# Element-wise work on VectorE alone, and the last factors of the MLP's input deferred, in a two-layer decoder step

## The chip, the core and the metric

The kernel runs on one core of a Trainium2 chip. The core has four engines that compute: TensorE multiplies matrices, VectorE, ScalarE and GpSimd work element by element; SyncE issues most transfers. Each engine takes its own instructions strictly in order and waits on semaphores for the others. The metric is the device time of one execution in microseconds (us). Before the change it is 1240.17 us, the median of three runs (1239.22 to 1240.53).

## The reference

One inference step of a small decoder with two layers, on 512 prompt tokens and 8 sample tokens (520 columns), model width 1024, MLP width 4096, all in float32:

```python
def rmsnorm(x, g): return x * rsqrt(mean(x * x) + EPS) * g
def sq_relu_mlp(x, g, w_up, w_down):
    return square(relu(rmsnorm(x, g) @ w_up)) @ w_down
# mixer A: input product -> six heads of chunkwise retention, group norm and swish gate,
#          beside attention over 256 memory tokens -> output product -> residual
# MLP 0; then one shared K/V product of the stream
# mixer B: input product -> twelve heads of sliding-window attention with sinks,
#          beside attention over memory tokens -> output product -> residual
# MLP 1; final RMSNorm
```

It returns the normed stream, the retention states and the key and value caches.

## The kernel before

The stream lies in the on-chip memory as eight blocks `xs[kt]` of 128 features by 520 tokens. Every product is computed on TensorE from split numbers: a float32 operand is cast to a shorter format on ScalarE (the high half, names in `h`), and the rest is subtracted on VectorE (the low half, names in `l`); three products of halves are added up in a bank. So before each product stands a pair of a ScalarE cast and a VectorE subtraction for the weights (`chunk`, lines 205 to 217; 128x1024 each, three buffers per kind) and for the input (`Pair.put`, lines 178 to 180; `cut`, line 251). A weight tile is fetched by SyncE once the buffer of the tile three earlier is free.

The program has four stages: mixer A, MLP 0, mixer B, MLP 1, with a norm at the start of each and one at the end. A norm squares on ScalarE, adds the squares up (line 384), sums over features on TensorE, takes the root by some eleven tiny VectorE steps (lines 357 to 365) and spreads the result through TensorE.

The MLP's input `xg` is split at once for the first four output blocks, which are computed by a plain product (`DIRECT = 2` pairs). For the rest the kernel uses a seven-product scheme on 2x2 halves: `operands` makes seven combinations of the input's quarter blocks (names `f0...`, `f1...`; the factors), and `seven` makes four sums of weight quarters for each pair of output blocks (names `u...s`, line 322, 128x512; the totals), 28 times in all.

Which engine does an element-wise step is written by hand in strings: `p` means GpSimd and `v` VectorE (`ENG_W` for the totals, `ENG_R` for the norms' adds, `POOL_N` for the window softmax, `TAIL_P` for the last multiplies). The multiplies of weights by a gain (line 214, `by`) and the multiply of `q` by decay (line 606) are always on GpSimd.

The order of each engine's instructions is not that of the code. The steps are recorded by generators in an order given by strings (`ORDER_A`, `ORDER_B`), and a scheduler then sorts each engine's instructions by a simulated time of readiness when the program is built. The sorted order is fixed; on the chip each engine follows it.

Names used below: `al` is the low half of mixer A's input; `ga` and `gt` are its gates, `rx` and `ry` TensorE's turned outputs of a head, `on` and `op` the normed head, `oah`, `oal` the halves of the gated outputs (`oah1` and `oal1` hold blocks 4 to 7; block 5 is head 5), `oa0` to `oa7` the output weights. In mixer B, `kv0` to `kv3` are the weights of the shared K/V, `qb0` to `qb7` those of the queries, a name such as `kv001` is the bank of tile 0, token half 1, and `kvb`, `qb1` are what the banks are evacuated to (line 421). `bms` are the norm's sums, `br` its spread result. `wp` are the window softmax's weights, six heads in turn (line 705). In the MLPs, `hid` also holds the split `xg`, `u` is an output block of the first product and `d` one of the second.

Of the kernel before, what the change touches and what calls it, by code (L numbers as in the profile page):

```python
# [33 lines left out]
DIRECT = 2  # L34
UK = KT // 2
# [11 lines left out]
ENG_UL = "vvvvvvvv"  # L47
ENG_R = dict(a='ppppvppv', m='pppppppv', f='vvvvvvvv', b='vvvvvpvv', y='vppppppv')
ENG_B = "pvvvvvvv"
ENG_W = "pvppppvp"  # L50
# [6 lines left out]
TAIL_P = (3, 5, 7)  # L57
STORES = ((1, 3, 5, 7), (0, 2, 4, 7))
KEEP = 4
POOL_W = (1, 4, 5)  # L60
POOL_N = (0, 1)
# [56 lines left out]
def build(tc, d, o):  # L118
    nc = tc.nc
    with ExitStack() as ctx:  # L120
# [39 lines left out]
        class Pair:  # L160
# [44 lines left out]
        def chunk(src, n, name, place=None, eng=nc.vector, by=None):  # L205
# [45 lines left out]
        def cut(op, j, src, eng):  # L251

            h, l = op[:, 0, j, :], op[:, 1, j, :]
            nc.scalar.copy(out=h, in_=src)
            eng.tensor_sub(out=l, in0=src, in1=f(h))

        def operands(name, g, scale, direct, norm):
# [12 lines left out]
            def put(i, j, src):  # L270
                if i not in op:
                    op[i] = half(f"{name}{i}", F32R, [P, 2, UK, EVEN])
                cut(op[i], j, src, nc.vector)

            for n, kt in enumerate(BY_PAIR):
                j = kt % UK
# [4 lines left out]
                if kt < UK:  # L281
                    first[j] = y
                    put(1, j, y[:, left])
                    combine(5, j, y[:, right], y[:, left], ALU.subtract)
                else:
                    b11, b12, b21, b22 = first[j][:, left], first[j][:, right], y[:, left], y[:, right]
                    t = combine(7, j, b22, b12, ALU.subtract)
                    t = combine(6, j, t, b11, ALU.add)
                    put(3, j, b22)
                    combine(4, j, b21, t, ALU.subtract)  # L290
                    put(2, j, b21)
            return op
# [819 lines left out]
```

## Time and profile before

| | us |
|---|---|
| median of three runs | 1240.17 |
| profiled execution | 1238.24 |
| its span (first to last instruction) | 1236.4 |
| TensorE busy | 1196.2 |
| VectorE busy | 833.4 |
| ScalarE busy | 534.6 |
| GpSimd busy | 229.4 |

The profile is of one execution, so that the sums below are made against its own span. Busy shares are means over stages that differ much: TensorE has nearly no idle time in the long product stretches and most of it at the boundaries of stages. The mean granted clock of TensorE over the span was 0.985 of full speed.

### The profile page before, as it was taken

To read this page: it belongs to the slowest core of one execution; us is meant where nothing else is said; L and a number is where in the kernel's file an instruction comes from. 1 tells how busy PE (TensorE), PEld (TensorE's weight loads), DVE (VectorE), ACT (ScalarE), POOL (GpSimd) and SP (SyncE) were. 2 spreads that over 40 slices of the span, in tenths; PEclk is the share of its full clock that TensorE was granted. 3 is DMA by queue.
4 is the path that set the end of the run, shared out by engine and by line. 5 is a ranking of instruction groups with operands and counts; after the bars stand their busy time and mean duration, and the time that the engine had idled before them with its cause. 6 is when DMAs were issued, how large, how long until landed. Compare 5 with 4: busy or idle time off the path is not lost. (4 is left out here: it accounts for less than half of the span.)

```text
span 1236.4 us, 23686 instructions
## 1 busy us (share of the span) xinstructions
PE 1196.2 (97%) x9718; PEld 1138.7 (92%) x9718; DVE 833.4 (67%) x1615; ACT 534.6 (43%) x999; POOL 229.4 (19%) x207
## 2 busy tenths in 40 slices
PE   8999999999999999999999998899799999999996
PEld 7999989999999999999999785579699999999996
DVE  7676777789766666675557558559796566666633
ACT  6232442355554444444324325455464444444532
POOL 2301100001312112121024114110222121121112
PEclk9999999999999999999999999899899999999998
DMA  8344622221223232232324354001132222323402
GB/s 304 112 151 168 217 77 72 88 86 71 73 97 120 86 116 91 97 106 75 121 99 143 107 163 141 30 1 68 36 103 103 82 107 86 120 86 104 140 32 69
DMA packets 43788, 128.25 MB, mean 104 GB/s; under 512 B 5112, under 2 KB 10368, under 8 KB 43552
## 3 DMA queue, kind: packets, MB, share of 16 engines
q1 hardware_dynamic: 41440, 119.80, 27.8%
q0 software_dynamic: 2240, 6.95, 1.5%
q8 instruction: 76, 1.25, 0.4%
q14 instruction: 32, 0.26, 0.1%
HBM read 117.65 MB, written 9.08 MB: 102 GB/s over the span
## 5 line engine op out<-in xcount | busy, mean ns | idle before, releaser
L438 DVE TENSOR_TENSOR xs<-d,xs 128x264 f32<-128x264 f32 (+1 forms) x128 | 54.0, 423 | 102.0 <-PE d L235 102.0
L235 PE MATMUL d<-hid,dw 128*128 128x256 f32 (+1 forms) x384 | 46.9, 283 | 0.0
L235 PEld LDWEIGHTS d<-hid,dw 128*128 128x128 f32 x384 | 46.3, 188 | 0.1
L830 ACT ACTIVATE u<-u 128x520 f32<-128x520 f32 x56 | 35.6, 636 | 21.5 <-DVE u L829 21.5
L639 POOL DMA_DIRECT2D out_ret_s<-s x12 | 6.9, 571 | 135.5 <-DVE s L638 102.8
L235 PE MATMUL ob<-obh,obw 128*128 128x256 f32 (+1 forms) x128 | 26.9, 297 | 2.4 <-ACT obh L179 1.6
L700 ACT ACTIVATE wp<-wp,wnm 128x256 f32<-128x256 f32 (+1 forms) x48 | 22.5, 469 | 12.6 <-DVE wes L697 8.6
L235 PEld LDWEIGHTS ob<-obh,obw 128*128 128x128 f32 x128 | 21.0, 193 | 5.0 <-ACT obh L179 3.0
L705 POOL TENSOR_SCALAR wp<-wp,wsm 128x256 f32<-128x256 f32 (+1 forms) x32 | 15.4, 498 | 54.8 <-ACT wp L700 28.5
L180 DVE TENSOR_TENSOR hid<-u,hid 128x520 fp32r<-128x520 f32 x32 | 23.3, 727 | 0.0
L829 DVE SCALAR_TENSOR_TENSOR u<-u,f0r 128x520 f32<-128x520 f32 x28 | 22.7, 811 | 0.4
L829 DVE SCALAR_TENSOR_TENSOR u<-u,f1r 128x520 f32<-128x520 f32 x28 | 22.7, 811 | 0.4
L524 ACT ACTIVATE p<-ms,nm 128x256 f32<-128x256 f32 x32 | 14.9, 476 | 18.5 <-DVE nm L522 16.8
L713 PEld LDWEIGHTS wt<-c,wp 128*128 128x128 f32 x84 | 9.8, 148 | 12.0 <-POOL wp L705 6.2
L179 ACT CAST hid<-u 128x520 fp32r<-128x520 f32 x32 | 20.1, 628 | 1.0
L713 PE MATMUL wt<-c,wp 128*128 128x128 f32 x84 | 15.7, 300 | 4.7 <-POOL wp L705 2.7
L235 PE MATMUL ob<-obl,obw 128*128 128x256 f32 (+1 forms) x64 | 18.1, 296 | 1.0 <-DVE obl L180 1.0
L522 DVE TENSOR_REDUCE nm<-ms 128x2 f32<-128x512 f32 x16 | 10.3, 685 | 11.8 <-PE ms L503 11.8
L180 DVE TENSOR_TENSOR obl<-wo,obh 128x128 fp32r<-128x128 f32 x24 | 6.9, 287 | 16.2 <-ACT obh L179 16.2
L503 PE MATMUL ws<-kvb,qb 64*128 64x256 f32 (+1 forms) x96 | 15.6, 407 | 1.2 <-DVE wp L690 0.6
L715 ACT COPY wpT<-wt 128x384 f32<-128x384 f32 x28 | 12.8, 479 | 8.2 <-PE wt L713 7.8
L690 DVE SCALAR_TENSOR_TENSOR wp<-cb,ws 128x256 f32<-128x256 f32 (+1 forms) x48 | 15.4, 375 | 0.1
(1997 smaller groups left out, 5124.6 us busy)
## 6 DMA issues: line engine op xcount, KB each, us to landing
kc<-in_mem_k SPq DMA_DIRECT2D x16, 256.0 KB, 4.1
vc<-in_mem_v SPq DMA_DIRECT2D x16, 256.0 KB, 4.4
s<-in_S SPq DMA_DIRECT2D x12, 256.0 KB, 4.9
out_ret_s<-s POOLq DMA_DIRECT2D x12, 256.0 KB, 2.5
xs<-in_xT SPq DMA_DIRECT2D x8, 260.0 KB, 4.3
memx<-in_memT SPq DMA_DIRECT2D x1, 1024.0 KB, 7.6
u004r<-in_w_up SPq DMA_DIRECT2D x2, 512.0 KB, 3.3
u006r<-in_w_up SPq DMA_DIRECT2D x2, 512.0 KB, 3.1
```

What stands on the lines that cost most here:

```text
L179: nc.scalar.copy(out=self.hi(kt, sl, rows), in_=src)
L180: eng.tensor_sub(out=self.lo(kt, sl, rows), in0=src, in1=f(self.hi(kt, sl, rows)))
L235: nc.tensor.matmul(t, w[:, ws], a(kt, HALVES[s]), start=kt == k[0] and m == 0, stop=kt == k[-1] and m == 2)
L438: nc.vector.tensor_add(out=x[mb][:, ts], in0=t, in1=x[mb][:, ts])
L503: i = m()
L524: nc.scalar.activation(out=t[:, b, :], in_=s[hh][:, b, :], func=AF.Exp, bias=nm[:, b:b + 1], accum_out=sm[:, b:b + 1])
L690: nc.vector.scalar_tensor_tensor(out=pv[:, j, :], in0=cb["nd"][:, k0:], scalar=float(SLOPES[6 * kb + j]), in1=sv[j // 3][j % 3], op0=ALU.m ...
L700: nc.scalar.activation(out=pv[:, j, :], in_=pv[:, j, :], func=AF.Exp, bias=nm[:, j:j + 1], accum_out=sm[:, j:j + 1])
L705: (nc.gpsimd if j % 3 in POOL_N else nc.vector).tensor_scalar(out=pv[:, j, :], in0=pv[:, j, :], scalar1=sm[:, j:j + 1], scalar2=1.0, op0=A ...
L713: nc.tensor.transpose(t[:, i * P:i * P + P], p[:, 3 * hh + i, kk * P:kk * P + P], ident)
L829: nc.vector.scalar_tensor_tensor(out=u[i], in0=u[i], scalar=0.0, in1=r[0], op0=ALU.max, op1=ALU.mult)
L830: nc.scalar.square(out=u[i], in_=u[i])
```

## The change

Two things change. All element-wise work of GpSimd goes to VectorE, with one exception: of the six heads of a window softmax, which GpSimd (four) and VectorE (two) scaled, VectorE now scales four and ScalarE two. GpSimd keeps memsets and the issue of its output transfers. The strings that chose engines are removed. Then `operands` returns the factors of its last two pairs (four blocks) as a generator, and the MLP's `up` takes one step of it behind each of the first two plain output blocks.

```diff
+LATE = 2
-ENG_UL = "vvvvvvvv"
-ENG_R = dict(a='ppppvppv', m='pppppppv', f='vvvvvvvv', b='vvvvvpvv', y='vppppppv')
-ENG_B = "pvvvvvvv"
-ENG_W = "pvppppvp"
-TAIL_P = (3, 5, 7)
-POOL_W = (1, 4, 5)
-POOL_N = (0, 1)
+ACT_N = (2, 5)
...
                 if by:
                     w = raw.rearrange("p (k c) -> p k c", k=KT)
-                    nc.gpsimd.tensor_tensor(out=w, in0=w, in1=gains[:, GAINS.index(by), :].unsqueeze(2).to_broadcast([P, KT, n // KT]),
+                    nc.vector.tensor_tensor(out=w, in0=w, in1=gains[:, GAINS.index(by), :].unsqueeze(2).to_broadcast([P, KT, n // KT]),
                                             op=ALU.mult)
...
+            def factors(j, upper, lower):
+                b11, b12, b21, b22 = (t[:, c] for t in (upper, lower) for c in (left, right))
+                put(1, j, b11)
+                combine(5, j, b12, b11, ALU.subtract)
+                t = combine(7, j, b22, b12, ALU.subtract)
+                t = combine(6, j, t, b11, ALU.add)
+                put(3, j, b22)
+                combine(4, j, b21, t, ALU.subtract)
+                put(2, j, b21)
+
+            later = []
             for n, kt in enumerate(BY_PAIR):
...
+                later.append(y)
+                if n < KT - 2 * LATE and n % 2:
+                    factors(n // 2, *later)
+                    later = []
+            return op, (factors(UK - LATE + i, *later[2 * i:2 * i + 2]) for i in range(LATE))
...
             def total(i, x0, x1, alu):
-                engine(ENG_W, i, turn).tensor_tensor(out=s[i], in0=x0, in1=x1, op=alu)
+                nc.vector.tensor_tensor(out=s[i], in0=x0, in1=x1, op=alu)
...
-                    engine(ENG_R[self.name[0]], 0 if self.direct else kt).tensor_add(out=acc, in0=acc, in1=sq)
+                    nc.vector.tensor_add(out=acc, in0=acc, in1=sq)
...
                 for j in range(6):
-                    (nc.gpsimd if j % 3 in POOL_N else nc.vector).tensor_scalar(
-                        out=pv[:, j, :], in0=pv[:, j, :], scalar1=sm[:, j:j + 1], scalar2=1.0, op0=ALU.mult, op1=ALU.mult)
+                    if j in ACT_N:
+                        nc.scalar.mul(out=pv[:, j, :], in_=pv[:, j, :], mul=sm[:, j:j + 1])
+                    else:
+                        nc.vector.tensor_scalar(out=pv[:, j, :], in0=pv[:, j, :], scalar1=sm[:, j:j + 1], scalar2=None, op0=ALU.mult)
...
-            op = operands(f"f{l}", f"mlp{l}", scale, xg, m)
+            op, late = operands(f"f{l}", f"mlp{l}", scale, xg, m)
...
                     hid.put(n, u)
+                    next(late, None)
                     yield
...
-                (nc.vector if s and kt not in TAIL_P else nc.gpsimd).tensor_mul(out=y, in0=y, in1=r)
+                nc.vector.tensor_mul(out=y, in0=y, in1=r)
```

The moves change the sorted order on every engine. Three places follow. The first is TensorE at the end of mixer A, behind the turned outputs of head 5 (`rx5`, `ry5`). Before:

```order
L667 MATMUL ry5_2914<-c_77,op5_2906 128x128
L235 MATMUL oa001_3215<-oah0_2276,oa0h_3184 128x264
L235 MATMUL oa001_3215<-oal0_2278,oa0h_3184 128x264
L667 MATMUL ry5_2914<-c_77,op5_2906 128x128
L235 MATMUL oa001_3215<-oah0_2276,oa0l_3185 128x264
L235 MATMUL oa001_3215<-oah0_2276,oa0h_3184 128x264
L235 MATMUL oa001_3215<-oal0_2278,oa0h_3184 128x264
L235 MATMUL oa001_3215<-oah0_2276,oa0l_3185 128x264
```

After, at the same place:

```order
L226 MATMUL oa400_3247<-oal1_1215,oa4h_3242 128x256
L226 MATMUL oa400_3247<-oah1_1213,oa4l_3243 128x256
L661 MATMUL rx5_2913<-c_77,on5_2905 128x128 x4
L661 MATMUL ry5_2914<-c_77,op5_2906 128x128 x2
L226 MATMUL oa000_3189<-oah1_1213,oa0h_3184 128x256
L226 MATMUL oa001_3215<-oah1_1213,oa0h_3184 128x264
L226 MATMUL oa400_3247<-oah1_1213,oa4h_3242 128x256
L226 MATMUL oa000_3189<-oal1_1215,oa0h_3184 128x256
```

Before, 31 matmuls that need other blocks follow the second `ry5`; now the last block's matmuls of three banks, which need head 5's output, follow at once. The second place is VectorE at the start of mixer B, behind the norm's last step `ry5`. Before:

```order
L365 SCALAR_TENSOR_TENSOR ry5_7952<-rqt_7956,rqu_7955 104x5
L400 TENSOR_TENSOR rz5_10326<-ry5_7952 104x5
L217 TENSOR_TENSOR kv3l_8316<-kv3r_8314,kv3h_8315 128x1024
L421 SCALAR_TENSOR_TENSOR kvb_7823<-kv000_7987,br_7968 128x256
L426 SCALAR_TENSOR_TENSOR qb1_7822<-qb1_7822,br_7968 128x520 x2
```

After:

```order
L359 SCALAR_TENSOR_TENSOR ry5_7952<-rqt_7956,rqu_7955 104x5
L205 TENSOR_TENSOR qb2r_8654<-qb2r_8654,gains_73 128x1024
L394 TENSOR_TENSOR rz5_10282<-ry5_7952 104x5
L415 SCALAR_TENSOR_TENSOR kvb_7823<-kv000_7987,br_7968 128x256
L415 SCALAR_TENSOR_TENSOR kvb_7823<-kv100_8166,br_7968 128x256
L420 SCALAR_TENSOR_TENSOR qb1_7822<-qb1_7822,br_7968 128x520 x2
```

`kv3l` has moved ahead of the norm, and the multiply of `qb2`'s weights by the gain, which was GpSimd's, now stands ahead of the evacuation of `kv000`. TensorE's sums of the norm, `bms`, stood inside the product of `kv000` before, and stand three matmuls into that of `kv100` now. The third place is VectorE at the start of MLP 1, ahead of the low half of the last block of `xg` (`f1xg7`). Before:

```order
L180 TENSOR_TENSOR hid1_10110<-f1xg3_10225,hid1_10110 128x520
L255 TENSOR_TENSOR f11_10117<-f1xg3_10225,f11_10117 128x260
L384 TENSOR_TENSOR f1acc_10111<-f1acc_10111,f1sq6_10229 128x520
L255 TENSOR_TENSOR f14_10147<-f1t41_10183,f14_10147 128x260
L266 TENSOR_TENSOR f1t62_10213<-f1t72_10209,f1xg2_10189 128x260
L255 TENSOR_TENSOR f15_10122<-f1t52_10198,f15_10122 128x260
L255 TENSOR_TENSOR f17_10134<-f1t72_10209,f17_10134 128x260
L322 TENSOR_TENSOR u104s0_10556<-u104s0_10556,u104r0_10549 128x512
L180 TENSOR_TENSOR hid1_10110<-f1xg7_10238,hid1_10110 128x520
```

After:

```order
L171 TENSOR_TENSOR hid1_10110<-f1xg3_10203,hid1_10110 128x520
L246 TENSOR_TENSOR f11_10124<-f1xg3_10203,f11_10124 128x260
L316 TENSOR_TENSOR u104s0_10556<-u104r1_10550 128x512
L378 TENSOR_TENSOR f1acc_10111<-f1acc_10111,f1sq6_10207 128x520
L316 TENSOR_TENSOR u104s1_10557<-u104r0_10549,u104r1_10550 128x512
L246 TENSOR_TENSOR f14_10147<-f1t41_10183,f14_10147 128x260
L257 TENSOR_TENSOR f1t62_10327<-f1t72_10323,f1xg2_10189 128x260
L246 TENSOR_TENSOR f15_10129<-f1t52_10319,f15_10129 128x260
L246 TENSOR_TENSOR f17_10134<-f1t72_10323,f17_10134 128x260
L171 TENSOR_TENSOR hid1_10110<-f1xg7_10210,hid1_10110 128x520
```

One total of the next product stood ahead of that low half, and needed GpSimd's two before it; now two totals stand there, both VectorE's own, and the factors keep their places.

## Rows read from the trace of the kernel before

**Rows 1.** The page's first lines: span, then busy time of each engine.

```profile
span 1236.4 us, 23686 instructions
...
PE 1196.2 (97%) x9718; PEld 1138.7 (92%) x9718; DVE 833.4 (67%) x1615; ACT 534.6 (43%) x999; POOL 229.4 (19%) x207
```

**Rows 2.** Three stretches: length, busy us (instructions) per engine, granted clock, DMA share, GB/s.

```profile
345.00:640.00 295.00, 294.95 (x2460) 294.74 (x2459) 186.44 (x240) 125.12 (x183) 52.89 (x37) 1.00 0.28 99
740.00:840.00 100.00, 86.77 (x585) 63.95 (x584) 63.59 (x200) 51.11 (x174) 23.74 (x35) 0.93 0.16 53
840.00:895.00 55.00, 46.65 (x348) 45.03 (x347) 48.41 (x104) 29.03 (x59) 7.92 (x4) 0.91 0.16 58
```

**Rows 3.** The waits of TensorE: instruction, releaser, us in total, times, longest.

```profile
PE u L235 <- DVE hid L180: 6.1, 2, 4.1
PE wt L713 <- POOL wp L705: 2.7, 5, 1.9
...
PE u110a L300 <- DVE u110l L317: 0.9, 1, 0.9
...
PE qm L235 <- DVE al L248: 0.7, 2, 0.4
```

**Rows 4.** Line 322 on VectorE: ns shortest, median, longest, then its start.

```profile
L322 DVE TENSOR_TENSOR u026s<-u026r,u026s x1: 680/680/680, 489.7 to 489.7; 128x512 f32<-128x512 f32 x1
...
L322 DVE TENSOR_TENSOR u104s<-u104s,u104r x1: 1741/1741/1741, 871.3 to 871.3; 128x512 f32<-128x512 f32 x1
```

**Rows 5.** Timeline, start of mixer B: start, us, instruction, [idle before <-releaser].

```profile
662.03 0.99 PE L394 MATMUL bms<-c,bacc 128*104 128x1 f32 x10
...
666.59 1.05 ACT L216 CAST kv3h<-kv3r 128x1024 fp32r<-128x1024 f32 x1 [5.42 <-issue]
...
668.34 1.22 DVE L217 TENSOR_TENSOR kv3l<-kv3r,kv3h 128x1024 fp32r<-128x1024 f32 x1
...
669.48 0.42 DVE L421 SCALAR_TENSOR_TENSOR kvb<-kv,br 128x256 f32<-128x256 f32 x1
...
669.95 0.39 PE L235 MATMUL kv<-bh,kv1h 128*128 128x264 f32 x1
```

**Rows 6.** Timeline of VectorE, start of MLP 1.

```profile
869.38 0.76 DVE L255 TENSOR_TENSOR f<-f1t,f 128x260 fp32r<-128x260 f32 x2
871.30 1.74 DVE L322 TENSOR_TENSOR u104s<-u104s,u104r 128x512 f32<-128x512 f32 x1 [1.16 <-POOL u104s L322]
872.96 0.69 DVE L180 TENSOR_TENSOR hid<-f1xg,hid 128x520 fp32r<-128x520 f32 x1
873.58 1.85 DVE L255 TENSOR_TENSOR f<-f1xg,f 128x260 fp32r<-128x260 f32 x2
```

**Rows 7.** Timeline, one window softmax.

```profile
814.40 0.85 DVE L705 TENSOR_SCALAR wp<-wp,wsm 128x256 f32<-128x256 f32 x2
814.55 1.94 POOL L705 TENSOR_SCALAR wp<-wp,wsm 128x256 f32<-128x256 f32 x4 [1.11 <-DVE wsm L703]
...
815.15 0.33 PE L713 MATMUL wt<-c,wp 128*128 128x128 f32 x1 [1.88 <-POOL wp L705]
```

**Rows 8.** Two stretches at half clock, columns as in Rows 2.

```profile
799.30:806.20 6.90, 6.43 (x32) 4.28 (x30) 5.75 (x25) 1.53 (x7) 0.00 (x0) 0.51 0.00 0
...
874.40:884.70 10.30, 9.03 (x41) 8.10 (x40) 9.52 (x29) 3.80 (x7) 0.39 (x1) 0.50 0.30 102
```

**Rows 9.** Timeline, the last multiplies.

```profile
1228.81 3.44 DVE L1023 TENSOR_TENSOR xs<-xs,y1r 128x264 f32<-128x264 f32 x5 [1.22 <-ACT y1r L411]
```

**Rows 10.** Timeline, end of mixer A.

```profile
252.21 0.27 PE L667 MATMUL ry<-c,op 128*128 128x128 f32 x1
...
254.18 0.70 DVE L180 TENSOR_TENSOR oal<-gt,oah 128x520 fp32r<-128x520 f32 x1 [0.69 <-ACT oah L179]
```

**Rows 11.** DMA issues, 664 to 675 us: transfer, KB, median us to landing.

```profile
qb2r<-in_w_in_b SPq DMA_DIRECT2D x1, 512.0 KB, 3.3
```

**Rows 12.** The waits of GpSimd, columns as in Rows 3.

```profile
POOL u126s L322 <- DMA u126r<-in_w_up: 17.3, 1, 17.3
```

More of the change, by code (lines that the diff above doesn't have):

```diff
@@ L176, in lo, with put @@
                 return self._at("l", kt)[rows, sl]
-            def put(self, kt, src, sl=slice(0, TT), rows=slice(0, P), eng=nc.vector):
+            def put(self, kt, src, sl=slice(0, TT), rows=slice(0, P)):
                 nc.scalar.copy(out=self.hi(kt, sl, rows), in_=src)
-                eng.tensor_sub(out=self.lo(kt, sl, rows), in0=src, in1=f(self.hi(kt, sl, rows)))
+                nc.vector.tensor_sub(out=self.lo(kt, sl, rows), in0=src, in1=f(self.hi(kt, sl, rows)))
         gains = cp.tile([P, len(GAINS), KT], F32, name="gains")
@@ L202, in gain, with chunk @@
             return gains[:, GAINS.index(name), kt:kt + 1]
-        def chunk(src, n, name, place=None, eng=nc.vector, by=None):
+        def chunk(src, n, name, place=None, by=None):
             raw = wp.tile([P, n], F32, name=f"{name}r", tag="wr", bufs=BUFS_W["wr"])
@@ L213, in fill @@
                     w = raw.rearrange("p (k c) -> p k c", k=KT)
-                    nc.gpsimd.tensor_tensor(out=w, in0=w, in1=gains[:, GAINS.index(by), :].unsqueeze(2).to_broadcast([P, KT, n // KT]),
+                    nc.vector.tensor_tensor(out=w, in0=w, in1=gains[:, GAINS.index(by), :].unsqueeze(2).to_broadcast([P, KT, n // KT]),
                                             op=ALU.mult)
                 nc.scalar.copy(out=wh[:, s], in_=raw[:, s])
-                eng.tensor_sub(out=wl[:, s], in0=raw[:, s], in1=f(wh[:, s]))
+                nc.vector.tensor_sub(out=wl[:, s], in0=raw[:, s], in1=f(wh[:, s]))
             return (wh, wl), fill
@@ L249, in split, with cut @@
                 out=a.lo(kt), in0=x[kt], scalar=gain(g, kt), in1=f(a.hi(kt)), op0=ALU.mult, op1=ALU.subtract)
-        def cut(op, j, src, eng):
+        def cut(op, j, src):
             h, l = op[:, 0, j, :], op[:, 1, j, :]
             nc.scalar.copy(out=h, in_=src)
-            eng.tensor_sub(out=l, in0=src, in1=f(h))
+            nc.vector.tensor_sub(out=l, in0=src, in1=f(h))
         def operands(name, g, scale, direct, norm):
@@ L280, in operands @@
                 norm.add(n, x[kt])
[L281 to L292, printed above, removed]
+                later.append(y)
[3 more added lines that the diff above has]
+            return op, (factors(UK - LATE + i, *later[2 * i:2 * i + 2]) for i in range(LATE))
         def times(t, w, op, more=False):
@@ L301, in times, with seven @@
                                      stop=j == nj - 1 and m == 2, skip_group_check=more)
-        def seven(src, op, u, name, turn):
+        def seven(src, op, u, name):
             n = UK * P
@@ L316, in parts @@
                 nc.scalar.copy(out=h[:, c], in_=t)
[L317 removed]
+                nc.vector.tensor_sub(out=l[:, c], in0=t, in1=f(h[:, c]))
                 for i, k in enumerate(ids):
@@ L826, in up @@
                     u = [blk(f"u{l}{g}{n}{i}", tag="u") for i in range(2)]
-                    seven([d["w_up"][l, g * FK + n + i] for i in range(2)], op, u, f"u{l}{g}{n}", n // 2)
+                    seven([d["w_up"][l, g * FK + n + i] for i in range(2)], op, u, f"u{l}{g}{n}")
                     for i in range(2):
@@ L953, in layer_b @@
             for kt in range(KT):
-                b.put(kt, x[kt], eng=engine(ENG_B, kt))
+                b.put(kt, x[kt])
             m = rms("b", "wp")
@@ L1003, in project_out @@
                     t = half(f"obw{n}", F32R, [P, 2, KT * P]) if n < KEEP else None
-                    ahead.append(weights(*src(mb), t if t is None else [t[:, 0], t[:, 1]], nc.gpsimd if n in POOL_W else nc.vector))
+                    ahead.append(weights(*src(mb), t if t is None else [t[:, 0], t[:, 1]]))
                 t = part(f"ob{mb}", s)
```

8 lines of the change are left out of this document (2 added, 6 removed).

## The prediction

> **What bounds the kernel now.** I read the page's totals first: the span is 1236.4 us and TensorE is busy for 1196.2 of it [rows 1]. VectorE at 67% and GpSimd at 19% can therefore matter only where TensorE waits, or where its clock is down. The table by stretch says where that is: between 345 and 640 us TensorE works 294.95 of 295 us, while from 740 to 840 it works 86.77 of 100 and from 840 to 895 46.65 of 55 [rows 2]. The waits of TensorE name the cause: 6.1 us for the low halves of `hid` that VectorE computes (line 180), 2.7 us for the softmax weights `wp` that GpSimd scales (line 705), 0.9 us for a low half of `u110` (line 317), 0.7 us for `al` at the start [rows 3]. So the change can gain where VectorE or GpSimd ends last, some 25 us in all, and it can lose where VectorE's queue, which runs in order, gets something new in front of what TensorE needs.
>
> The profiled execution took 1238.24 us, 1.84 above its span and 1.93 below the median of 1240.17. I take each step as a difference in the profiled execution and add the sum to the median.
>
> **Work moved to VectorE.** The totals of the products are 84 GpSimd instructions of 128x512; the 28 that VectorE has already take 0.68 us undisturbed [rows 4] and, as its instructions overlap by some 0.08, hold its queue for 0.6: 84 x 0.6 = 50 us. For the twelve gain multiplies of 128x1024 the nearest row is a subtraction of that size, 1.22 us and 1.14 of queue [rows 5]: 14 us. The other sixty or so are smaller, some 22 us by size. VectorE thus gets about 86 us, 833 + 86 = 919 (74%) as the upper end. Against it stands what goes. A VectorE instruction that starts under a GpSimd one is stretched: a total takes 1.74 in place of 0.68 [rows 4], the pair at 873.58 took 1.85 where the pair at 869.38 took 0.76 [rows 6]. That is about 1.07 each time, and if 50 to 100 of the 169 moved instructions meet one, it is 53 to 107 us. VectorE's total will stay near where it was. In the long stretches it has 186.44 of 295 us now [rows 2], with 33 more totals 206, which TensorE's 294.95 cover; I cost the totals of such stretches at nothing. Without that cover each call of three would cost 1.8 us.
>
> **Deferred factors.** For the four last blocks the recorded order changes, but the scheduler sorts by readiness: on VectorE the factors of the last pairs stand in the same places among their neighbours in both programs. Their own effect is zero.
>
> **Gains, place by place.**
> - Start: the two waits for `al` go, -0.6 of the 0.7 [rows 3].
> - Window softmax: six heads are scaled after each of eight normalisations. Now GpSimd does four in series, 1.94 us from 814.55, and VectorE two in 0.85; TensorE waits 1.88 for one of them at 815.15 [rows 7]. After, VectorE does four in about 1.3 and ScalarE two, which stand behind the exponentials of the next head group. The 2.7 us of waits go in part, and some of the stretch at half clock behind them (6.9 us at 0.51 between 799.3 and 806.2 [rows 8]) may. I take -3.0; the ends are +1 (ScalarE's two come late) and -7.
> - Start of MLP 1: the low half `hid` at 872.96, for which TensorE waits 4.10 us, stands behind a total that waits 1.16 for GpSimd and takes 1.74 [rows 3, 6]. After, two plain totals of 0.6 stand there: 1.16 + 1.66 - 1.2 = 1.6 earlier. Two more totals stand behind it against 1.09 of stretch at 873.58, and the norm's chain ends about 1.3 earlier. TensorE's work there is at half clock (0.50 from 874.4 to 884.7 [rows 8]) and not the later one: -1.3, ends 0 and -4.
> - 895 to 920, where the wait of 0.9 for `u110` stands [rows 3]: -0.7, as three totals more than before stand ahead of it but no stretch. Last multiplies: eight on VectorE at 0.35 from 1228.81 end at 1231.65, where five, stretched, end at 1232.25 [rows 9]: -0.5.
>
> Sum of gains: -0.6 - 3.0 - 1.3 - 0.7 - 0.5 = -6.1.
>
> One rule of the Trainium skill speaks against this. At the start of MLP 1 VectorE is without idle time but for the wait of 1.16 [rows 6]. "Perfetto Trace Analysis", section Optimizing Scalar/DVE Operations, says that where VectorE is saturated, offloading even to GpSimd may make sense, and adds that the shared port may undo that. By the first half taking the work back would cost the four totals, 4 x 0.6 = +2.4 in place of -1.3, and the sum would be +2.3 in place of -1.4; by the second half the stretch goes with GpSimd's work, and the 1.74 against 0.68 [rows 4] agrees with that half.
>
> **Losses, place by place.**
> - End of mixer A. The gates of the last heads are now computed earlier, so TensorE has less to do behind head 5. Before, 31 matmuls of 0.12 us (294.95 / 2460 [rows 2]) stand between the second `ry` and the first matmul that needs head 5's gated output; its low half ends at 254.88, 2.4 us behind `ry`'s end at 252.48 [rows 10], under 31 x 0.12 = 3.7. After, the matmuls behind `ry` are those that need block 5. They start once `oah` is there, and the fourth of them needs the low half: 2.4 - 3 x 0.12 = about +2.0. Ends: 0.5 (if TensorE comes late to `ry`) and 3.
> - Start of mixer B. The multiplies by the gain now stand in VectorE's queue and wait there for their weights. That of `qb2` stands ahead of the evacuation of the first `kv` tile, which frees the bank for the last product of `kv1`. The chain: the buffer for `qb2` is free when `kv3l` is done. `kv3h` (1.05) started at 666.59, as the product of `kv0` was through; the statistics' ten matmuls (0.99) no longer stand inside that product, so now at 665.6. Then `kv3l` 1.2, the transfer 3.3 [rows 11], the multiply 1.14, the evacuation 0.42: 665.6 + 1.05 + 1.2 + 3.3 + 1.14 + 0.42 = 672.7 for the product which started at 669.95 [rows 5], when TensorE has nothing else to do: +2.7. Ends: 0 (the evacuation has what it needs only shortly before) and 5, since `qb3`, `qb4` and `qb5` can hold evacuations in the same way; I take none of those, as 6 to 8 other instructions stand between them.
>
> Sum of losses: +4.7.
>
> **Result.** -6.1 + 4.7 = -1.4: 1240.17 - 1.4 = about 1238.8.
>
> **Rivals.**
> 1. VectorE's queue waits on transfers everywhere (slower). One mechanism: an instruction that waits for its raw weights now holds all of VectorE. GpSimd waited 17.3 us for `u126r` [rows 12], and nothing was queued behind that; VectorE meets such waits at 28 calls and at the multiplies of `qb3` to `qb5`. Before, the evacuations in VectorE's queue just ahead of this one ended near the landing, so I expect 0 to 0.3 there. If TensorE's banks cover none of that, the price is 28 x 0.3 = 8 us; the sum is -1.4 + 8 and, with one such multiply in three uncovered, 1247 to 1249.5; I take 1247. It decides from the point where TensorE shows gaps between 345 and 640 us or between 675 and 720. For it: in-order queues. Against: VectorE is idle for 108 of the 295 us [rows 2].
> 2. The window part and the two MLP starts give more (faster). If the clock stays up once the gaps are short, the 6.9 and 10.3 us at half clock [rows 8] give back up to 3.4 and 2 us, and a third instead of a quarter of the 13.2 us idle in 740 to 840 [rows 2] goes. Then -6.1 becomes -6.1 - 5.4 - 1.1 = -12.6, the losses are half: -12.6 + 2.4 = about 1230. For it: the stretched instructions lie mostly there. Against: most of those waits are for ScalarE or for chains that the change leaves alone.
> 3. The move doesn't relieve VectorE: the stretch is not GpSimd's doing and stays. Then VectorE is at 74%, the starts of both MLPs, where it is saturated, get 2.4 us each, and -1.3, -0.7 and half of the -3.0 fall away: -1.4 + 4.8 + 3.5 = +6.9, about 1247. Against: the same instruction takes 0.68 without and 1.74 [rows 4] with GpSimd busy.
>
> **Chances.** A change of this kernel can be told from none from about 0.2%, 2.5 us. The forecast of no such change has 0.34; the second rival 0.36; the first 0.20; the third 0.10. The forecast's own spread reaches over both edges: of its 0.34 I give 0.04 to faster. So faster 0.40, same 0.30, slower 0.30. The range, from the second rival to the first, is 1229 to 1248, a microsecond beyond each, with some 0.1 outside at either end; the forecast's own is 1235 to 1242.
>
> **What would show it.** In the changed kernel's profile: GpSimd busy under 25 us and VectorE between 800 and 860; 128x512 totals on VectorE at 0.68 throughout (against rival 3). A gap of TensorE near 253 of about 2 us, released by `oah` or `oal`, and one near 670 of about 2.7, released by an evacuation; no gaps of it in 345 to 640 and 920 to 1200 (against rival 1). No wait of TensorE for line 705 on GpSimd, the stretch 740 to 840 shorter by 2 to 4 us. In MLP 1 the wait of 4.10 for `hid` under 3. If those two gaps are absent, I am too slow by up to 5 us; if the long stretches have gaps, I am too fast.

## The result, and the profile after

The changed kernel takes 1249.88 us (median of four runs, 1246.23 to 1250.16) where the kernel before takes 1239.88 in the same comparison: a ratio of 1.0070 with a 95% interval of 1.0056 to 1.0085. It is slower, by 7 to 10.5 us, and outside the range forecast. The profiled execution took 1249.91 us, 11.67 more than that of before.

The first lines of the page after; columns as in [rows 1].

```profile
span 1248.1 us, 23531 instructions
...
PE 1203.8 (96%) x9718; PEld 1144.4 (92%) x9718; DVE 850.3 (68%) x1766; ACT 539.0 (43%) x1015; POOL 21.4 (2%) x40
```

TensorE runs the same 9718 matmuls and is busy 7.6 us longer; its idle time (span less busy) grew from 40.2 to 44.3, by 4.1. So two thirds of the loss is slower matmuls, not waiting. VectorE's total is up by only 17 us and GpSimd's is down by 208.

The stretches of [rows 2] after, and one of MLP 1:

```profile
345.00:640.00 295.00, 295.00 (x2460) 295.00 (x2459) 192.51 (x281) 126.03 (x185) 0.00 (x0) 1.00 0.28 99
740.00:840.00 100.00, 83.41 (x566) 61.21 (x565) 65.51 (x221) 55.06 (x189) 5.48 (x8) 0.92 0.22 71
840.00:895.00 55.00, 50.66 (x358) 46.59 (x357) 44.46 (x98) 29.66 (x65) 0.00 (x0) 0.87 0.16 51
920.00:1200.00 280.00, 280.00 (x2334) 280.00 (x2333) 192.25 (x278) 131.39 (x196) 0.00 (x0) 1.00 0.29 102
```

The long stretches have no idle time at all. The loss lies at the boundaries of stages, as the waits of TensorE show, columns as in [rows 3]. Two of them before, which [rows 3] leaves out:

```profile
PE wt L713 <- ACT wpT L715: 2.0, 6, 0.9
...
PE wss L744 <- DMA kwc<-in_swa_k: 0.4, 1, 0.4
```

After:

```profile
PE wt L709 <- ACT wpT L711: 4.4, 5, 2.3
PE u L226 <- DVE hid L171: 3.6, 2, 2.0
PE wss L740 <- DMA kwc<-in_swa_k: 3.4, 1, 3.4
...
PE bmt L403 <- DVE ry L359: 2.3, 1, 2.3
...
PE oa L226 <- ACT oah L170: 1.8, 1, 1.8
PE kv L226 <- DVE kvb L415: 1.8, 1, 1.8
```

The waits for GpSimd are gone and that for `hid` is down from 6.1 to 3.6. New are those of `bmt`, `oa` and `kv`. Two have grown: the one for `kwc`, from 0.4 to 3.4, and the one for `wpT`, the copies by ScalarE of the turned softmax weights, from 2.0 to 4.4.

Behind those stalls TensorE runs at half clock. Four such stretches after, columns as in [rows 2]; the granted clock is the third number from the right:

```profile
258.30:261.80 3.50, 3.50 (x18) 3.50 (x18) 3.15 (x6) 2.52 (x4) 0.00 (x0) 0.51 0.02 5
678.20:681.60 3.40, 3.20 (x14) 3.20 (x15) 2.62 (x9) 0.00 (x0) 0.00 (x0) 0.50 0.00 0
780.60:787.40 6.80, 3.44 (x19) 3.09 (x20) 2.03 (x16) 4.65 (x20) 1.88 (x3) 0.50 0.75 253
883.00:896.60 13.60, 11.45 (x52) 10.58 (x50) 13.36 (x36) 4.79 (x9) 0.00 (x0) 0.50 0.24 76
```

Over the whole span the stretches at half clock (1.2 GHz) make 51.1 us where they made 37.7 before. In the first of them 18 matmuls take 3.50 us; at the 0.12 us that one takes in the long stretches (295 / 2460) it would be 2.16, so it costs 1.3.

**Place by place.** The first table compares the ends of the same matmuls in the two profiled executions, part by part: the last one that reads `qkv00h`, `oa7h`, `d010h`, `kv1l`, `ob7h` and `d110h`, and the end of the span. The second gives the same for the experiments (us against before). Each column compares one execution with one; late0, which turns out to be the changed kernel over again, shows how far two executions of the same instructions differ in a part: up to 1.5 us. The profiled execution isn't always a typical one: those of before_qw and qb_norm_pool are the slowest of their runs. The ratios are of all runs.

| part, ends with | forecast | after |
|---|---|---|
| start, `qkv00h` | -0.6 | -2.1 |
| mixer A, `oa7h` | +2.0 | +5.1 |
| start of MLP 0, `d010h` | 0 | +1.2 |
| start of mixer B, `kv1l` | +2.7 | +5.6 |
| queries and window, `ob7h` | -3.0 | +4.8 |
| start of MLP 1, `d110h` | -2.0 | -1.3 |
| rest, end of the span | -0.5 | -1.6 |
| sum | -1.4 | +11.7 |

| kernel | start | mixer A | MLP 0 | start of B | window | MLP 1 | rest | ratio of times [95%] |
|---|---|---|---|---|---|---|---|---|
| late0 | -1.7 | +5.6 | +1.3 | +6.5 | +3.9 | -2.8 | -1.4 | 1.0061 [1.0049, 1.0073] |
| qw_pool | -1.9 | +0.2 | -0.3 | +7.9 | +3.0 | -1.3 | -1.5 | 1.0024 [1.0013, 1.0036] |
| by_pool | -2.6 | +5.5 | +1.3 | +1.2 | +3.1 | -1.4 | -1.6 | 1.0015 [1.0004, 1.0026] |
| qw_by_pool | -2.4 | +0.7 | -0.3 | +1.0 | +4.2 | -1.6 | -1.4 | 0.9981 [0.9973, 0.9990] |
| qb_norm_pool | -1.7 | +0.3 | +1.3 | +0.8 | -0.3 | -1.3 | -1.0 | 0.9947 [0.9931, 0.9963] |
| qb_obw_pool | -1.9 | +0.1 | +1.3 | +0.7 | +2.5 | -2.9 | -1.4 | 0.9970 [0.9958, 0.9982] |
| qb_norm_obw_pool | -1.9 | +0.2 | +1.1 | +1.5 | -0.2 | -1.5 | -1.4 | 0.9957 [0.9941, 0.9973] |
| qb_dve6 | -2.7 | 0.0 | -0.3 | +0.8 | +0.5 | -1.3 | -1.6 | 0.9958 [0.9946, 0.9970] |
| before_qw | -0.5 | +3.8 | -0.4 | +1.3 | +0.8 | +2.7 | +0.1 | 1.0038 [1.0026, 1.0050] |
| before_by_dve | +0.1 | 0.0 | -0.3 | +2.4 | -0.6 | +1.3 | +0.1 | 1.0014 [1.0002, 1.0025] |
| before_norm | -0.2 | +0.3 | +0.1 | +1.4 | +3.1 | -0.1 | -0.1 | 1.0031 [1.0019, 1.0043] |
| before_totals | -0.2 | +0.4 | -0.3 | +0.7 | +1.2 | -1.5 | -0.2 | 0.9981 [0.9970, 0.9992] |

The first eight are the changed kernel with a part undone or altered, the last four the kernel before with one part alone.

**The end of mixer A**, timeline after, columns as in [rows 5]:

```profile
255.08 0.38 PE L661 MATMUL ry<-c,op 128*128 128x128 f32 x2
...
256.63 0.62 ACT L170 CAST oah<-gt 128x520 fp32r<-128x520 f32 x1 [0.77 <-DVE gt L933]
...
257.29 0.70 DVE L171 TENSOR_TENSOR oal<-gt,oah 128x520 fp32r<-128x520 f32 x1 [0.69 <-ACT oah L170]
...
257.31 0.51 PE L226 MATMUL oa<-oah,oa0h 128*128 128x256 f32 x2 [1.85 <-ACT oah L170]
```

In [rows 10] work stood behind `ry`; now TensorE waits 1.85 us for `oah`. The half clock from 258.3 on, above, comes right behind.

**The start of mixer B**, VectorE after:

```profile
655.08 1.23 DVE L205 TENSOR_TENSOR kv2r<-kv2r,gains 128x1024 f32<-128x1024 f32 x1 [2.73 <-DMA kv2r<-in_w_kv]
...
665.03 1.23 DVE L205 TENSOR_TENSOR kv3r<-kv3r,gains 128x1024 f32<-128x1024 f32 x1 [1.37 <-DMA kv3r<-in_w_kv]
...
671.19 1.22 DVE L205 TENSOR_TENSOR qb1r<-qb1r,gains 128x1024 f32<-128x1024 f32 x1 [1.44 <-DMA qb1r<-in_w_in_b]
...
675.67 0.17 DVE L359 SCALAR_TENSOR_TENSOR ry<-rqt,rqu 104x5 f32<-104x5 f32 x1
676.71 1.23 DVE L205 TENSOR_TENSOR qb2r<-qb2r,gains 128x1024 f32<-128x1024 f32 x1 [0.87 <-DMA qb2r<-in_w_in_b]
...
677.93 0.75 DVE L415 SCALAR_TENSOR_TENSOR kvb<-kv,br 128x256 f32<-128x256 f32 x2
```

and TensorE there:

```profile
675.89 0.66 PE L403 MATMUL bmt<-c,ry 104*128 104x104 f32 x5 [2.30 <-DVE ry L359]
...
678.40 0.59 PE L226 MATMUL kv<-bh,kv1h 128*128 128x264 f32 x1 [1.85 <-DVE kvb L415]
```

VectorE's whole queue waits for raw weights at `kv2r`, `kv3r`, `qb1r` and `qb2r`. The first three stand ahead of the norm's root, so `ry` and with it `bmt` come late; the last stands ahead of the evacuation `kvb`. TensorE stalls twice.

**The window part.** The whole of it, from the end of `kv1l` to that of `ob7h`, columns as in [rows 2]; first before, then after:

```profile
674.41:856.52 182.11, 168.88 (x1219) 134.21 (x1219) 116.15 (x341) 84.97 (x266) 36.67 (x50) 0.96 0.26 85
```

```profile
684.27:871.16 186.89, 170.10 (x1219) 133.85 (x1219) 121.51 (x363) 91.41 (x283) 7.64 (x11) 0.95 0.26 83
```

TensorE's idle time in it (length less busy) grew from 13.2 to 16.8 us, and its half clock, summed from the trace, from 13.7 to 17.1. The place of one of the long waits, late in it, all engines:

```profile
834.29 0.51 ACT L694 ACTIVATE wp<-wp,wnm 128x256 f32<-128x256 f32 x1 [3.47 <-DVE wes L691]
...
836.86 0.49 ACT L694 ACTIVATE wp<-wp,wnm 128x256 f32<-128x256 f32 x1
...
837.35 0.83 ACT L711 COPY wpT<-wt 128x384 f32<-128x384 f32 x2
...
837.86 0.55 PE L709 MATMUL wt<-c,wp 128*128 128x128 f32 x3 [2.27 <-ACT wpT L711]
837.91 0.88 DVE L702 TENSOR_SCALAR wp<-wp,wsm 128x256 f32<-128x256 f32 x3
838.08 0.91 ACT L700 ACTIVATE wp<-wp,wsm 128x256 f32<-128x256 f32 x2
```

ScalarE's queue holds six exponentials of one head group (line 694, 834.29 to 837.35) ahead of the copy of `wpT` that TensorE wants for another; the two scalings (line 700) stand behind the copies. TensorE waits 2.27 us, and has half clock from 838.6 to 842.0. For the heads that ScalarE scales, TensorE (its weight loads) waits only 0.5 us in the whole part. Two more long waits there are 3.4 for `kwc` and 2.3 for `obh`, both listed above.

**The start of MLP 1**, VectorE after:

```profile
882.63 0.68 DVE L316 TENSOR_TENSOR u104s<-u104r 128x512 f32<-128x512 f32 x1
...
883.85 0.68 DVE L316 TENSOR_TENSOR u104s<-u104r,u104r 128x512 f32<-128x512 f32 x1
...
885.81 0.69 DVE L171 TENSOR_TENSOR hid<-f1xg,hid 128x520 fp32r<-128x520 f32 x1
```

The two totals take 0.68 us and wait for nobody, where one took 1.74 and waited 1.16 [rows 6]. TensorE's wait for this low half is 1.60 (at 886.56), was 4.10. Over the part, up to the end of `d110h`, TensorE's idle time fell from 9.2 to 5.6 us, while its half clock grew from 10.2 to 17.1: that is why the part gains no more than 1.3.

### The profile page after: what moved, and what is told of

It is laid out like the page before. It is cut to its first block, busy times and chain, and to the rows that moved or that the text cites. A ratio compares the mean times of both kernels' runs of the same rounds, so it can differ in the third digit from the quotient of the medians.

```text
span 1248.1 us, 23531 instructions
## 1 busy us (share of the span) xinstructions
PE 1203.8 (96%) x9718; PEld 1144.4 (92%) x9718; DVE 850.3 (68%) x1766; ACT 539.0 (43%) x1015; POOL 21.4 (2%) x40
## 4 chain that ended last, share of the span: by engine, by line
PE 86%; DVE 8%; DMA 3%; ACT 2%; issue 1%; SPq 0%; DVEq 0%; ACTq 0%
PE d L226 28%; PE qkv L226 8%; PE oa L226 4%; PE qb L226 3%; PE ga L226 3%; PE u L226 3%; PE kv L226 1%; PE ob L226 1%; PE ms L497 1%; PE memv L482 1%; PE memk L471 1%; ACT wp L694 1%; DVE wp L684 1%; DVE f L246 1%; PE mt L530 1%
## 5 line engine op out<-in xcount | busy, mean ns | idle before, releaser
L826 DVE SCALAR_TENSOR_TENSOR u<-u,f1r 128x520 f32<-128x520 f32 x28 | 19.5, 697 | 0.4
L826 DVE SCALAR_TENSOR_TENSOR u<-u,f0r 128x520 f32<-128x520 f32 x28 | 19.5, 696 | 0.4
L497 PEld LDWEIGHTS ws<-kvb,qb 64*128 64x128 f32 x96 | 10.1, 203 | 5.5 <-DVE wp L684 3.2
L631 DVE TENSOR_TENSOR kvs<-rb,ks 128x512 f32<-128x512 f32 x12 | 8.2, 686 | 9.6 <-PE rb L629 9.6
```

What stands on the lines that cost most here:

```text
L497: i = m()
L826: nc.vector.scalar_tensor_tensor(out=u[i], in0=u[i], scalar=0.0, in1=r[0], op0=ALU.max, op1=ALU.mult)
```

## The experiments

Each ran 5 to 12 times beside the kernel before. The first four undo parts of the change; their edits are shown against the changed kernel.

**late0** defers no factors.

```diff
-LATE = 2
+LATE = 0
```

> The changed kernel without the deferral (LATE = 0): all factors are made in the first loop. Theory: the scheduler sorts by readiness and the deferral has no effect of its own, so the time is that of the changed kernel within 1.5 us. Rival: deferring frees VectorE at both MLP starts, and without it the kernel is 2 us or more slower than the changed one.

Measured: 1248.35 us; its interval overlaps that of the changed kernel. The instructions stand in the same order on all five engines and differ in buffer numbers alone. The deferral does nothing. The two are thus one program for the engines, and where their rows in the table differ (by 0.9 at the start of mixer B and in the window, by 1.5 at the start of MLP 1) only the execution differs; half clock in that last part is 17.1 us in one and 13.7 in the other.

**qw_pool** puts the multiply of `q` by decay (six of 128x384) back on GpSimd.

```diff
-            nc.vector.tensor_mul(out=qw, ...
+            nc.gpsimd.tensor_mul(out=qw, ...
```

> The changed kernel with one edit undone: the six multiplies of q by the decay (qw) are GpSimd's again. Theory: the end of mixer A is lost to the sorted order alone, because these six in VectorE's queue move the gates ahead; with them back the 31 matmuls stand behind ry5 again, TensorE's gap of 1.85 near 255 and the half clock behind it (3.4 us, worth 1.7) are gone, the kernel is 3 to 5 us faster than the changed one and still 4 to 7 slower than the one before. Rival (the load on VectorE in mixer A is what costs): the order changes but the time lost there stays within 1 us.

Measured: 1244.09 us, by the ratios 5.7 us faster than the changed kernel and 3.0 slower than before, which is more than expected. The loss in mixer A goes from +5.1 to +0.2 and the +1.2 behind it is gone too; that at the start of mixer B stays.

**by_pool** puts the twelve gain multiplies back on GpSimd.

```diff
-                    nc.vector.tensor_tensor(out=w, in0=w, in1=gains[...
+                    nc.gpsimd.tensor_tensor(out=w, in0=w, in1=gains[...
```

> The changed kernel with one edit undone: the twelve multiplies of weights by a gain are GpSimd's again. Theory: the start of mixer B is lost because VectorE stands idle for transfers in its own queue (2.73, 1.37, 1.44 and 0.87 us before kv2r, kv3r, qb1r and qb2r), so the gaps of 2.30 and 1.85 near 675 go, and the order of transfers in the window part is the old one too (last kwc before ob7r), so the gap of 3.41 for kwc goes: 7 to 10 us faster than the changed kernel, within 2 us of the one before. Rival (the window part is lost to the softmax's new engines): only the 5.6 us at mixer B come back, the 4.6 us between 740 and 840 stay lost.

Measured: 1242.90 us, by the ratios 6.8 us faster than the changed kernel. The start of mixer B goes from +5.6 to +1.2, and mixer A keeps its +5.5. With the multiplies on GpSimd the fetch of `kwc` is no longer late (TensorE waits 0.70 for it in place of 3.41), yet the window part still loses 3.1, as the rival had it: most of what the part lost doesn't hang on that wait.

**qw_by_pool** undoes both.

```diff
-            nc.vector.tensor_mul(out=qw, ...
+            nc.gpsimd.tensor_mul(out=qw, ...
...
-                    nc.vector.tensor_tensor(out=w, in0=w, in1=gains[...
+                    nc.gpsimd.tensor_tensor(out=w, in0=w, in1=gains[...
```

> The changed kernel with both undone: qw and the gain multiplies are GpSimd's again, all else is on VectorE. Theory: both losses go and the gains at the start (2 us) and in MLP 1 (1.3 to 1.8) stay, so it is 2 to 5 us faster than the kernel before. Rival (the totals on VectorE cost as much as they give): no faster than the kernel before, within 2 us.

Measured: 1238.63 us, 0.19% (2.4 us) faster than before, at the low end of what was expected. Both losses are gone; the window part still costs +4.2. What is left there are the softmax's scaling and the low halves of the output weights `obw`, of which three were GpSimd's. The next four, all built on qw_by_pool and shown against it, tell these apart.

**qb_norm_pool** scales the six heads as before.

```diff
-                    if j in ACT_N:
-                        nc.scalar.mul(out=pv[:, j, :], in_=pv[:, j, :], mul=sm[:, j:j + 1])
-                    else:
-                        nc.vector.tensor_scalar(...
+                    (nc.gpsimd if j % 3 in POOL_N else nc.vector).tensor_scalar(...
```

> qw and the gain multiplies on GpSimd as in qw_by_pool, and the window softmax's scaling as before (four heads on GpSimd, two on VectorE, none on ScalarE). Theory A: the 4.3 us lost between 740 and 840 come from ScalarE's two heads, which stand behind the next head group's exponentials; then they come back and this is 4 to 6 us faster than the kernel before. Theory B: they come from the three low halves of output weights (ob1, ob4, ob5, 1.22 us each, names n of 1, 4, 5) that stand in VectorE's queue ahead of the softmax chains; then 3 us or more of them stay lost and it is within 1.5 us of qw_by_pool.

Measured: 1233.90 us, 0.53% faster than before, the lowest ratio of all (the intervals of qb_norm_obw_pool and qb_dve6 overlap with it). The window's loss is gone (-0.3). Its page:

```profile
PE 1197.6 (97%) x9718; PEld 1141.3 (92%) x9718; DVE 841.7 (68%) x1732; ACT 533.8 (43%) x999; POOL 67.8 (5%) x90
```

GpSimd keeps 67.8 us: mainly the multiplies of `qw`, those by the gain and four heads of each scaling. The other work that the change took from it, 162 us by [rows 1], went to VectorE, which is busy only 8 us longer than before.

**qb_obw_pool** leaves the scaling as changed, with three low halves of `obw` on GpSimd.

```diff
+POOL_W = (1, 4, 5)
...
-                nc.vector.tensor_sub(out=wl[:, s], in0=raw[:, s], in1=f(wh[:, s]))
+                eng.tensor_sub(out=wl[:, s], in0=raw[:, s], in1=f(wh[:, s]))
...
-                    ahead.append(weights(*src(mb), t if t is None else [t[:, 0], t[:, 1]]))
+                    ahead.append(weights(*src(mb), t if t is None else [t[:, 0], t[:, 1]], nc.gpsimd if n in POOL_W else nc.vector))
```

> qw and the gain multiplies on GpSimd as in qw_by_pool, and the low halves of three output weights of mixer B (a subtraction of 128x1024 each) on GpSimd as before; the softmax's scaling as in the changed kernel. Theory B: the window part gets back 3 us or more, and it is 4 to 6 us faster than the kernel before. Theory A: it gets back less than 1.5 us.

Measured: 1237.49 us; the window keeps +2.5 of +4.2. It gets back 1.7, which lies between what the two theories say, so that the low halves may have a share, but they aren't the main cause.

**qb_norm_obw_pool** has both of these edits.

```diff
-                    ahead.append(weights(*src(mb), t if t is None else [t[:, 0], t[:, 1]]))
+                    ahead.append(weights(*src(mb), ..., nc.gpsimd if n in POOL_W else nc.vector))
...
-                    if j in ACT_N:
...
+                    (nc.gpsimd if j % 3 in POOL_N else nc.vector).tensor_scalar(...
```

> Both of those back: on VectorE are only the totals, the norms' adds, the first low half of mixer B and the last multiplies. Both theories: the window part is that of the kernel before, so the gains at the start (1.7 us) and in MLP 1 (1.3 to 1.8 us) stand alone, -3 to -4.5 us against the kernel before. If it is slower than the better of the two others, the engines in the window part matter less than the order into which each version is sorted.

Measured: 1235.70 us, not told apart from qb_norm_pool: the intervals overlap. Which engine takes those low halves matters little once the scaling is as before.

**qb_dve6** keeps GpSimd out of the scaling, but gives VectorE all six heads and ScalarE none.

```diff
-ACT_N = (2, 5)
+ACT_N = ()
```

> qw_by_pool with all six heads of the window softmax scaled on VectorE, none on ScalarE. Theory A1: the window part is lost to ScalarE's two heads, which stand behind other exponentials; then the stretch 740 to 855 gets back 2.5 us or more and the kernel is 4.5 us or more faster than the one before, as with GpSimd. Theory A2: it is lost to VectorE's queue, which holds the softmax chains of several head groups; then it is no faster than qw_by_pool, 1 to 3 us under the kernel before.

Measured: 1234.06 us, 0.42% faster than before. The window costs +0.5 in place of qw_by_pool's +4.2, though VectorE has more to do. This kernel at the place that was shown after:

```profile
821.44 0.46 ACT L711 COPY wpT<-wt 128x384 f32<-128x384 f32 x1
821.80 0.51 ACT L694 ACTIVATE wp<-wp,wnm 128x256 f32<-128x256 f32 x1
...
821.95 0.55 PE L709 MATMUL wt<-c,wp 128*128 128x128 f32 x3 [1.29 <-ACT wpT L711]
```

The copy now stands among the exponentials and not behind them; the wait is 1.29, and the clock stays up there. That giving ScalarE two heads causes the loss is thus shown: the two programs differ in this edit alone, and their intervals lie apart. How it does so is not shown. The window part of qw_by_pool, then that of this kernel, columns as in [rows 2]:

```profile
673.42:859.78 186.36, 169.86 (x1220) 134.13 (x1219) 118.36 (x360) 90.93 (x282) 13.78 (x15) 0.95 0.26 83
```

```profile
672.29:854.92 182.63, 166.65 (x1219) 131.78 (x1219) 122.28 (x376) 84.99 (x266) 14.13 (x15) 0.98 0.26 84
```

Of the 3.7 us between them only 0.5 is waiting of TensorE (16.5 against 16.0 idle). The other 3.2 is busy time: 17.1 us at half clock in one and 6.8 in the other. And in qw_by_pool, where the copy stands behind the same six exponentials, TensorE waits only 0.61 for it. Whether the 0.9 us of a pair of scalings or the other order of the queues changes where the clock falls was not tried apart.

The last four add one part of the change to the kernel before.

**before_qw**

```diff
-            nc.gpsimd.tensor_mul(out=qw, ...
+            nc.vector.tensor_mul(out=qw, ...
```

> The kernel before with one edit: the six multiplies of q by the decay (128x384) on VectorE. They are 6 x 0.5 = 3 us of VectorE's time. Theory: it is the order into which TensorE's gates are sorted and not these 3 us that costs; TensorE shows the gap of about 1.85 near 255 with half clock behind it, and the kernel is 3 to 5 us slower than the one before. Rival (the changed kernel's other edits are needed for the loss): within 1.5 us of the kernel before.

Measured: 1244.61 us. Six multiplies move, and mixer A loses +3.8. TensorE there:

```profile
256.64 0.38 PE L667 MATMUL ry<-c,op 128*128 128x128 f32 x2
...
258.87 0.51 PE L235 MATMUL oa<-oah,oa0h 128*128 128x256 f32 x2 [1.85 <-ACT oah L179]
```

The same stall of 1.85 with nothing left to do behind `ry`: this edit alone re-sorts the gates. The half clock that was expected behind it does not follow here, and mixer A loses 1.3 less than in the changed kernel; the start of MLP 1, with 20.5 us at half clock where before has 10.2, loses 2.7.

**before_by_dve**

```diff
-                    nc.gpsimd.tensor_tensor(out=w, in0=w, in1=gains[...
+                    nc.vector.tensor_tensor(out=w, in0=w, in1=gains[...
```

> The kernel before with one edit: the twelve gain multiplies on VectorE. Theory: VectorE stands idle for the weights' transfers at the start of mixer B, TensorE gets gaps of 2 to 4 us there with half clock behind, and the last kwc is issued behind ob7r: 4 to 8 us slower than the kernel before. Rival (it takes the lighter load of the changed kernel's neighbours to bring the multiplies forward): less than 2 us slower.

Measured: 1241.99 us. VectorE waits for the same transfers:

```profile
660.90 1.22 DVE L214 TENSOR_TENSOR kv3r<-kv3r,gains 128x1024 f32<-128x1024 f32 x1 [1.41 <-DMA kv3r<-in_w_kv]
...
668.01 1.23 DVE L214 TENSOR_TENSOR qb1r<-qb1r,gains 128x1024 f32<-128x1024 f32 x1 [1.51 <-DMA qb1r<-in_w_in_b]
```

By the ratio that is 1.7 us slower, not the 4 to 8 expected; the rival's bound of 2 holds. TensorE's two stalls are 1.71 (`bmt`) and 0.98 (`kvb`), with no half clock behind them: +2.4, of which 0.6 comes back before the end of the window. So the move brings the stalls, and their size depends on what else stands in the queue.

**before_norm** has the scaling of the change: VectorE four heads, ScalarE two.

```diff
-                    (nc.gpsimd if j % 3 in POOL_N else nc.vector).tensor_scalar(...
+                    if j in ACT_N:
+                        nc.scalar.mul(out=pv[:, j, :], in_=pv[:, j, :], mul=sm[:, j:j + 1])
+                    else:
+                        nc.vector.tensor_scalar(...
```

> The kernel before with one edit: the window softmax scaled by VectorE (four heads) and ScalarE (two) instead of GpSimd (four) and VectorE (two). Theory: 2 to 4 us slower than the kernel before, all of it between 740 and 855. Rival (the loss needs the output weights' low halves on VectorE too): within 1.5 us.

Measured: 1243.52 us; the window loses +3.1. One of its waits, all engines:

```profile
754.52 3.32 POOL L217 TENSOR_TENSOR obw<-ob4r,obw 128x1024 fp32r<-128x1024 f32 x1 [18.02 <-ACT obw L216]
755.28 0.91 ACT L706 ACTIVATE wp<-wp,wsm 128x256 f32<-128x256 f32 x2
...
755.75 3.02 DVE L708 TENSOR_SCALAR wp<-wp,wsm 128x256 f32<-128x256 f32 x4
...
758.04 2.27 PE L715 MATMUL wt<-c,wp 128*128 128x128 f32 x10 [2.39 <-DVE wp L708]
```

Here a second cause mixes in, which the changed kernel doesn't have: under GpSimd's 3.32 us the four scalings take 3.02 where they take 1.14 alone. So the +3.1 isn't ScalarE's alone. Nor is it waiting: TensorE's idle time in the part is 12.8 us against 13.2 before, and its half clock 23.9 against 13.7.

**before_totals** moves the 84 totals to VectorE.

```diff
-ENG_W = "pvppppvp"
+ENG_W = "vvvvvvvv"
```

> The kernel before with one edit: all 84 totals of GpSimd on VectorE. Theory: the long stretches keep TensorE without gaps, the start of MLP 1 gains 1.3 to 2 us and nothing else moves: 1 to 3 us faster than the kernel before. Rival (VectorE waits for the raw weights in its own queue and TensorE gets gaps in the long stretches): slower than the kernel before by 2 us or more.

Measured: 1238.04 us, 0.19% faster. The long stretches, columns as in [rows 2]:

```profile
345.00:640.00 295.00, 295.00 (x2460) 295.00 (x2460) 189.00 (x273) 124.31 (x183) 6.74 (x4) 1.00 0.30 99
920.00:1200.00 280.00, 280.00 (x2336) 280.00 (x2335) 181.69 (x265) 126.28 (x191) 4.43 (x6) 1.00 0.29 99
```

Half the change's instructions, and TensorE has no idle time in either stretch. VectorE's busy time in the first stretch grows by 2.6 us for 33 more instructions: what the totals cost, the stretch gives back. The gain is at the start of MLP 1 (-1.5), where TensorE waits 2.43 for the low half in place of 4.10, with as much half clock as before.

By themselves the four parts are worth +4.7, +1.7, +3.8 and -2.4 us (ratios above, times 1240), together +7.9; the whole change is 8.7 by its ratio. That these are close doesn't show that the parts simply add up. The gain multiplies cost 1.7 alone, and undoing them in the changed kernel brings back 6.8; and the change has other moves (the norms' adds, low halves, the last multiplies), while the -2.1 at the start and the -1.6 at the end hardly show with any of the four alone.

## Why the prediction was wrong

**What held.** GpSimd is at 21.4 us and VectorE at 850.3, inside the bounds given. No total takes over 0.70 us, so the stretch was GpSimd's doing and the third rival is out. The long stretches have no gaps: VectorE does wait for the totals' weights, up to 1.3 us for `u024r`, and TensorE has no idle time there. The Trainium skill, "Perfetto Trace Analysis", Optimizing Scalar/DVE Operations, has both halves of this: by the first half taking the totals back should have cost 2.4 us at the saturated place, by the second it should not; before_totals, 0.19% faster, agrees with the second. The deferral is worth nothing. Both stalls foretold are there, 1.85 for `oah` and 1.85 for `kvb`; the wait of 4.10 in MLP 1 is 1.60, and that part's -1.3 stands against the -2.0 forecast, as half clock took back what the waits gave. The start gave more, -2.1 for -0.6: one of the four parts alone (before_qw) shows -0.5 there, the others stay within 0.2, and which of the other moved instructions bring it wasn't tried.

**The step that failed: the window softmax.** It was put at -3.0, with an upper end of +1 for "ScalarE's two come late". The part lost 4.8 in the changed kernel and 4.2 in qw_by_pool. The prediction let waits of 2.7 us go in part [rows 3], put new ones at nothing, and counted half clock only as something to win. In the changed kernel the waits for GpSimd went, but TensorE's idle time in the part grew by 3.6 us all the same, with 3.4 for `kwc`, 2.3 for `obh` and 2.27 for `wpT`, and half clock grew by 3.4. qb_dve6 and qb_norm_pool show from two sides that ScalarE's two heads bring the loss: without them the part is at +0.5 and -0.3. They don't bring it in the way of the upper end, for TensorE waits 0.5 us in all for the heads that ScalarE scales; between qw_by_pool and qb_dve6 it is mostly the clock, and why that stays up more without these heads is open. Of the 13.1 us between the forecast's sum and the profiled pair, this term is the largest, with 7.8. The Trainium skill, "Trainium Architecture — The Big Picture", The five engines, in one table, lists simple arithmetic among what ScalarE is not for. The rows agree as to time, 0.495 us a head (the median of its 16) against VectorE's 0.345, but TensorE's waits for those heads are too short to be the loss.

**Mis-sized: the end of mixer A**, +2.0, measured +5.1. The gap is the one foretold (1.85 for `oah` and 0.11 for `oal`). What was left out: 1.3 us of half clock behind it, and 0.9 at the memory tokens' products, where TensorE waits 0.48 for `mh` at 126.6. Some 0.9 more is spread over the part and wasn't traced. qw_pool and before_qw show that the six small multiplies bring nearly all of it.

**Mis-sized: the start of mixer B**, +2.7, measured +5.6. I followed one chain, `qb2` to `kvb`, and it came, at 1.85 us for the 2.7 forecast. I took none of the other multiplies, although `kv2`, `kv3` and `qb1` wait for transfers in the same queue, ahead of the norm's root: that is the stall of 2.30 at `bmt`. Then 3.4 us at half clock, in which 14 matmuls took 3.20 where 1.7 would do. by_pool shows the cause. The first rival's mechanism, VectorE's queue held by a transfer, was thus right at the gain multiplies and wrong at the totals.

**The common error** is that a stall of TensorE was priced as its own length. Behind stalls of about 2 us stood 3.4 to 6.8 us at 1.2 GHz in the changed kernel, and TensorE's busy time, with the same matmuls, grew by 7.6 of the 11.7 us. I had used the half clock only as a possible gain [rows 8].

**Not settled.** The +1.2 at the start of MLP 0 doesn't come from longer waits: the changed kernel and qw_pool have the same two stalls there, 1.22 and 0.98. Of the 12 us around them, first the changed kernel's row, then qw_pool's:

```profile
311.00:323.00 12.00, 9.80 (x69) 9.39 (x68) 6.42 (x20) 3.36 (x7) 0.00 (x0) 0.86 0.23 85
```

```profile
311.00:323.00 12.00, 11.38 (x95) 11.38 (x96) 8.18 (x15) 7.18 (x13) 0.00 (x0) 1.00 0.00 1
```

One has half clock and loses 1.5 us from there to the next product, the other has none and loses nothing. In the table the part is at +1.1 to +1.3 or at -0.4 to +0.1, and nothing between. The kernels of the first group have 3.4 us of half clock in the part, the others none. Which of the two a run gets was not found; it may be part of why the changed kernel's four runs span 1246.23 to 1250.16.

## What to carry to other kernels

Price a new stall of TensorE by its length and, as a second case, by the half clock that may follow it: here 1.3 to 1.5 us for each 3.4 us of it. An instruction that waits for a transfer is cheap on an engine that nobody waits for and dear at the head of one whose next instructions are a norm's root or an evacuation. That an instruction waits for no transfer doesn't make its move safe either: six small multiplies of `q` cost 4.7 us alone, because the program's scheduler re-sorted TensorE's instructions around them. The 84 totals, whose waits nobody felt, could move and gave 2.4. Before a small task goes to a third engine, read what stands ahead of it and behind it in that engine's new order: the idle share (ScalarE was idle for more than half of the time) doesn't tell.

## What was not expected of the hardware

At one point of the program (the start of MLP 0), with the same two stalls, some profiled executions show 3.4 us at a granted clock of 0.5 and others none. And an instruction of GpSimd and one of VectorE that run together can both lose: in before_norm four scalings took 3.02 us for 1.14, under a subtraction of 128x1024 that itself took GpSimd 3.32, where the same subtraction took 2.37 in the kernel before.
